# Forgetting attention with gate sums of keys only, fused maxima, late normalising and more units in flight

## The chip, the cores and the metric

The kernel runs on one core of one Trainium2 chip. The metric is the device time of one execution, in microseconds; three executions of the kernel before took 3905.02, 3905.59 and 3907.46 us. In the text PE is TensorE, DVE is VectorE, ACT is ScalarE, POOL is GpSimd, and SP is the queue that issues most DMAs.

## What is computed

The whole net is two blocks of two layers. Only one part is changed, the forgetting attention of the last layer: 512 tokens, 16 heads of width 64, causal, with a bias that is the difference of two running sums of a gate, F of the query's token and F of the key's.

```python
def forgetting_attention(h, w_q, w_o, k, v, F):
    q = (h @ w_q).reshape(b, s, B_HEADS, HEAD_DIM)
    def block(args):                      # 128 queries
        causal = q_pos[:, None] >= k_pos[None, :]
        decay = transpose(Fqb, (0, 2, 1))[..., None] - F_k[:, :, None, :]
        logits = einsum('bqhd,bkhd->bhqk', qb, k) * HEAD_DIM ** -0.5 + decay
        logits = where(causal, logits, -inf)
        p = softmax(logits, axis=-1)
        return einsum('bhqk,bkhd->bqhd', p, v)
    ...
    return o.reshape(b, s, B_WIDTH) @ w_o
```

Since the softmax runs over the keys, a term that depends on the query alone drops out of it.

## The kernel before

Activations lie with their channels on the partitions: a tile is 128 channels by 512 tokens. Large products take three matmuls for each 128 by 128 block of weights (`mm3`, lines 252 to 254): the weights are split into a rounded part `wh` (ACT, line 244) and the rest `wl` (DVE, line 245), the activations likewise. The split weights rotate through three buffers of four blocks each. `project` (line 361) is a generator: each step splits the weights of one output tile, 24 matmuls into one PSUM bank, and evacuates it.

The forgetting stage stands between two feed-forward parts. `norm2` makes its 8 input tiles (lines 323, 325 and 326). Then 8 pairs of heads follow. A pair has the query tile of its two heads, each on 64 partitions (`project`, evacuated on ACT at line 1415 as `q`), and four units, for the query blocks i = 3, 2, 1, 0, with 512, 384, 256 and 128 keys. At the first unit of a pair the gate sums of the keys are spread over all partitions, by four transposes (line 1470) and an ACT copy (line 1473, `fk`) per head.

A unit has `scores` and `values`. `scores` multiplies queries and keys (line 1427, the two heads in two banks), adds the gate sums (line 1432, DVE), adds the causal mask and takes the row maximum (line 1434, DVE), takes exponentials and their sums (line 1437, ACT), and normalises (lines 1438 and 1439, DVE). `values` transposes the weights on PE (`transposed`, lines 351 and 352, the copy on ACT), and multiplies them with the values (line 1454); the result of a pair gathers in one bank, `po`. `values` of a unit is written after `scores` of the next. After the 8 pairs, `out_project` multiplies the mixed tiles with the output weights.

The order on each engine is fixed when the program is built. A scheduler takes what it holds ready by its own costs, by the order of the code; `self.later()` gives the projections of the queries a lower priority than everything else. PSUM has eight banks: two with the tag `m` for projections, six with the tag `f` for all else. The three-matmul products here keep PE filled where heads leave gaps.

## Time and profile before

| | |
|---|---|
| median of three runs | 3905.59 us |
| span of the profiled execution, first to last instruction | 3901.2 us |
| PE busy, share of the span | 3663.6 us, 94% |
| DVE busy | 2172.9 us, 56% |
| ACT busy | 1445.6 us, 37% |
| POOL busy | 147.8 us, 4% |
| forgetting stage, first score matmul to end of the output projection | 3333.44 to 3514.33 us |
| in 3325 to 3515 us: DVE in line 1432, 1434, 1439 | 33.9, 30.2 and 24.5 us |
| in 3325 to 3515 us: ACT in line 1437, 352 | 35.5 and 26.1 us |

The page gives the span of the profiled execution and no time of its own beside it; the median lies 4.4 us above the span, which is what lies around the program. A granted clock of 1.00 is the full one of PE, 2.4 GHz, about half is its lower level of 1.2 GHz. A busy row of PE shows a matmul until its modelled end, while the next may start earlier, so the distance between two starts tells more than the length of a row.

### The profile page before, as it was taken

What the parts mean: (1) busy time and instruction counts of PE and PEld (TensorE: products, weight loads), DVE (VectorE), ACT (ScalarE), POOL (GpSimd) and SP (SyncE); (2) the same over time, 40 slices, a digit from 0 to 9 for tenths busy, and PEclk for the clock granted to TensorE, in tenths of its full rate; (3) what the DMA queues carried; (4) which work ended last, traced back from release to release, by engine and by line L of the source; (5) the groups of instructions that cost most, each with busy time, mean ns of one, the idle gap of its engine ahead of it and who ended that gap; (6) DMA issues with size and microseconds to landing.
All of it is one profiled execution on the core that took longest, in us unless ns stands there. A gap on an engine that the chain in (4) does not pass through costs nothing. (4 is left out here: it accounts for less than half of the span.)

```text
span 3901.2 us, 54964 instructions
## 1 busy us (share of the span) xinstructions
PE 3663.6 (94%) x21248; PEld 2659.1 (68%) x21248; DVE 2172.9 (56%) x5458; ACT 1445.6 (37%) x2827; POOL 147.8 (4%) x267
## 2 busy tenths in 40 slices
PE   7999998999899997988999998999989999999998
PEld 4777785333577775535888776788868888677887
DVE  5899874122688864215566665655643334764334
ACT  4566431111456631113233454323333233553222
POOL 0000000000000000000010000001100000000000
PEclk8999998999999997999999998999989999999999
DMA  5223254876433465995555321455522222012222
GB/s 203 70 80 101 77 196 167 327 275 259 156 111 109 135 215 199 356 356 179 194 194 189 113 76 54 142 193 205 191 80 97 96 94 95 33 52 79 97 102 81
DMA packets 154197, 588.04 MB, mean 151 GB/s; under 512 B 18048, under 2 KB 57256, under 8 KB 111952
## 3 DMA queue, kind: packets, MB, share of 16 engines
q1 hardware_dynamic: 113760, 442.43, 31.5%
q0 software_dynamic: 37872, 137.90, 10.5%
q10 hardware_dynamic: 2304, 4.20, 0.3%
q8 instruction: 167, 2.74, 0.3%
q14 instruction: 94, 0.77, 0.1%
HBM read 575.01 MB, written 9.46 MB: 150 GB/s over the span
## 5 line engine op out<-in xcount | busy, mean ns | idle before, releaser
L245 DVE TENSOR_TENSOR wl<-raw,wh 128x512 fp32r<-128x512 f32 (+1 forms) x826 | 558.3, 677 | 722.4 <-ACT wh L244 712.8
L244 ACT ACTIVATE wh<-raw 128x512 fp32r<-128x512 f32 (+1 forms) x826 | 512.1, 622 | 1203.2 <-PE m L253 835.1
L252 PE MATMUL m<-h,wh 128*128 128x512 f32 x1632 | 661.3, 406 | 30.6 <-DVE t L323 8.4
L253 PE MATMUL m<-h,wh 128*128 128x512 f32 x1632 | 658.3, 404 | 6.6 <-DVE h L326 5.2
L254 PE MATMUL m<-h,wl 128*128 128x512 f32 x1632 | 658.8, 404 | 1.1 <-DVE wl L245 1.1
L174 DVE SCALAR_TENSOR_TENSOR junk<-g,cb 128x512 bf16<-128x512 f32 (+1 forms) x440 | 374.1, 850 | 29.8 <-DMA g<-in_modT 17.5
L252 PEld LDWEIGHTS m<-h,wh 128*128 128x128 f32 x1632 | 315.4, 193 | 104.5 <-ACT h L325 19.1
L253 PEld LDWEIGHTS m<-h,wh 128*128 128x128 f32 x1632 | 313.8, 192 | 81.1 <-DVE h L326 16.3
L254 PEld LDWEIGHTS m<-h,wl 128*128 128x128 f32 x1632 | 313.9, 192 | 68.7 <-issue 6.9
L254 PE MATMUL m<-e,wl 128*128 128x512 f32 x832 | 325.7, 392 | 7.9 <-DVE wl L245 7.9
L252 PE MATMUL m<-e,wh 128*128 128x512 f32 x832 | 325.3, 391 | 0.5 <-ACT wh L244 0.5
L253 PE MATMUL m<-e,wh 128*128 128x512 f32 x832 | 324.9, 391 | 0.0
L252 PE MATMUL f<-h,wh 128*128 128x512 f32 x768 | 299.5, 390 | 0.0
L254 PE MATMUL f<-h,wl 128*128 128x512 f32 x768 | 299.1, 389 | 0.0
L253 PE MATMUL f<-h,wh 128*128 128x512 f32 x768 | 299.0, 389 | 0.0
L1106 PE MATMUL m<-raw,xg 128*64 128x512 f32 (+1 forms) x1264 | 258.5, 609 | 10.5 <-DMA raw<-in_exp_gu 10.5
L254 PEld LDWEIGHTS m<-e,wl 128*128 128x128 f32 x832 | 157.0, 189 | 40.9 <-DVE wl L245 8.3
L1106 PEld LDWEIGHTS m<-raw,xg 128*64 128x64 f32 (+1 forms) x1264 | 64.1, 126 | 175.0 <-issue 147.6
L252 PEld LDWEIGHTS m<-e,wh 128*128 128x128 f32 x832 | 157.2, 189 | 33.5 <-ACT wh L244 1.3
L253 PEld LDWEIGHTS m<-e,wh 128*128 128x128 f32 x832 | 157.0, 189 | 32.7
L252 PEld LDWEIGHTS f<-h,wh 128*128 128x128 f32 x768 | 144.5, 188 | 30.1 <-PE m L253 0.2
L254 PEld LDWEIGHTS f<-h,wl 128*128 128x128 f32 x768 | 144.3, 188 | 30.3 <-DVE wl L245 0.2
(455 smaller groups left out, 5170.0 us busy)
## 6 DMA issues: line engine op xcount, KB each, us to landing
raw<-in_exp_gu SPq DMA_DIRECT2D x98, 1024.0 KB, 6.6
raw<-in_ffn_in SPq DMA_DIRECT2D x88, 1024.0 KB, 4.8
g<-in_adaT POOLq DMA_DIRECT2D x144, 512.0 KB, 3.9
raw<-in_exp_dn SPq DMA_DIRECT2D x48, 1024.0 KB, 6.7
g<-in_modT POOLq DMA_DIRECT2D x80, 512.0 KB, 3.9
raw<-in_w_in SPq DMA_DIRECT2D x30, 1024.0 KB, 4.8
raw<-in_ffn_out SPq DMA_DIRECT2D x32, 896.0 KB, 4.6
raw<-in_ffn_out SPq DMA_DIRECT2D x16, 1024.0 KB, 4.7
```

The costliest lines, as they stand in the source:

```text
L174: self.paced(nc.vector.scalar_tensor_tensor(self.junk, before[0][:, js], 1.0, cb[:, js], op0=OP.mult, op1=OP.mult, accum_out=part[:, j:j + ...
L244: self.nc.scalar.activation(hi, src, AF.Copy)
L245: self.nc.vector.tensor_tensor(lo, src, hi.bitcast(F32), op=OP.subtract)
L252: nc.tensor.matmul(out, wh[k], hh[k], start=(first and k == ks[0]), stop=False)
L253: nc.tensor.matmul(out, wh[k], hl[k], start=False, stop=False)
L254: self.last = nc.tensor.matmul(out, wl[k], hh[k], start=False, stop=(last and k == ks[-1]))
L1106: self.nc.tensor.matmul(out[es, c:c + n], xg[:, es], t, start=start, stop=stop)
```

## The change

- The gate sum of the query's token is left out of the scores. What is added to a score is then minus the gate sum of the key, in a tile `bias` with two versions: plain, and with the causal triangle added to every block of 128 (the addition on GpSimd, line 1435). Each head has these in buffers that hold matrix-vector data in other stages (`g` and `cb`). `prepare` makes them, one pair ahead.
- One DVE instruction per part (line 1455) adds the bias to the scores out of PSUM and takes the maximum: one part without the triangle, one for the last 128 keys with it. A reduction (line 1457) joins the maxima of a unit's two heads, negated.
- The weights are not normalised. They are transposed as they are, and copied by ACT for one head (line 1477) and by DVE for the other (line 1475). The reciprocals of the sums of a whole pair are spread (line 1489, DVE), transposed by four matmuls (line 1493), copied (line 1496, ACT), and multiplied into the result of the pair (line 1498, DVE).
- PSUM: one bank `m`, four banks `s` for scores, two banks `f`, one bank `o` for the results.
- `values` stands two units behind `scores`; two projections are asked for before the loop, and one at the start of each pair.

```diff
-            with self.phase("forget", {"t": 3, "acc": 1, "q": 8, "fk": 3, "e": 4, "w": 3, "mix": 8}, {"m": 2, "f": 6}):
-                self.b2_consts()
+            with self.phase("forget", {"t": 4, "acc": 1, "q": 4, "fk": 2, "e": 6, "w": 4, "mix": 8},
+                            {"m": 1, "s": 4, "f": 2, "o": 1}):
...
+        def prepare(p):
+            for e in range(2):
+                b = self.bank()
+                for j in range(4):
+                    nc.tensor.transpose(b[:, j * 128:(j + 1) * 128],
+                                        self.Fq[:, j, 2 * p + e:2 * p + e + 1].to_broadcast([128, 128]), self.ident)
+                tag = ("g", "cb")[e]
+                t = bias[p, e] = self.gp.tile([128, 2, T], F32, tag=tag, name=tag)
+                nc.scalar.activation(t[:, 0], b, AF.Copy, scale=-1.0)
+                blocks = lambda u: u.rearrange("p (i m) -> p i m", m=128)
+                nc.gpsimd.tensor_tensor(blocks(t[:, 1]), blocks(t[:, 0]), tri.unsqueeze(1).to_broadcast([128, 4, 128]),
+                                        op=OP.add)
...
-                b = self.bank()
+                b = self.bank("s")
...
-                nc.vector.scalar_tensor_tensor(t[:, :n], fk[p, e][:, :n], self.Fq[:, i, hd:hd + 1], b[:, :n],
-                                               op0=OP.subtract, op1=OP.subtract, reverse1=True)
-                nc.vector.tensor_tensor_reduce(t[:, :n], t[:, :n], mask[:, 384 - 128 * i:512], 1.0, -3.0e38,
-                                               OP.add, OP.max, sm[:, 0:1])
-                nc.vector.tensor_scalar(sm[:, 1:2], sm[:, 0:1], -1.0, None, op0=OP.mult)
-                nc.scalar.activation(t[:, :n], t[:, :n], AF.Exp, bias=sm[:, 1:2], accum_out=sm[:, 2:3])
-                nc.vector.reciprocal(sm[:, 3:4], sm[:, 2:3])
-                nc.vector.tensor_scalar(t[:, :n], t[:, :n], sm[:, 3:4], None, op0=OP.mult)
-                P[p, i, e] = t
+                t = P[p, i, e] = self.tmp("e")
+                for part, cs in ((0, slice(0, n - 128)), (1, slice(n - 128, n))):
+                    if part or i:
+                        nc.vector.tensor_tensor_reduce(t[:, cs], b[:, cs], bias[p, e][:, part, cs], 1.0, -3.0e38, OP.add,
+                                                       OP.max, sm[:, 2 * e + part:2 * e + part + 1])
+            nc.vector.tensor_reduce(sm[:, 4:6], sm[:, 0:4].rearrange("p (e j) -> p e j", j=2), axis=AX.X, op=OP.max,
+                                    negate=True)
+            for e in range(2):
+                t = P[p, i, e]
+                nc.scalar.activation(t[:, :n], t[:, :n], AF.Exp, bias=sm[:, 4 + e:5 + e], accum_out=sums[p][:, i, e:e + 1])
...
+            if i == 1:
+                r = self.small(8).rearrange("p (i e) -> p i e", e=2)
+                nc.vector.reciprocal(r, sums[p])
+                sums[p] = self.tmp("t").rearrange("p (i e d) -> p i e d", e=2, d=64)
+                nc.vector.tensor_copy(sums[p], r.unsqueeze(3).to_broadcast([128, 4, 2, 64]))
             if i == 0:
+                b = self.bank()
+                for j in range(4):
+                    nc.tensor.transpose(b[:, j * 128:(j + 1) * 128], sums[p][:, j].rearrange("p e d -> p (e d)"),
+                                        self.ident)
+                rb = self.tmp("t")
+                nc.scalar.activation(rb, b, AF.Copy)
                 mix.append(self.tmp("mix"))
-                nc.scalar.activation(mix[p], po[p], AF.Copy)
+                nc.vector.tensor_mul(mix[p], po.pop(p), rb)
...
+        project_q(2)
+        prepare(0)
         units = [(p, i) for p in range(8) for i in (3, 2, 1, 0)]
+        ahead = 2
...
-        self.out_project(a["b_o"], mix, gate, st)
+        self.out_project(a["b_o"], mix, gate, st, "msfs")
```

What the change does to the order on the engines, at the places where a pair of heads begins. First PE in the kernel before, at the start of the pair of `q_28117`. In the names, `s` or `f` are score banks, `e` weights, `w` transposed weights, `m` projections, and a wait names the engine that ends it.

```order
L1470 MATMUL f_28126<-ident_75,Fq_24295 128x128
L1427 MATMUL f_28133<-k_24444,q_28117 128x512
L1427 MATMUL f_28135<-k_24444,q_28117 128x512 [waits PE_49]
L351 MATMUL f_28154<-ident_75,e_28054 128x128 [waits DVE_49,PE_49]
L351 MATMUL f_28158<-ident_75,e_28062 128x128 [waits DVE_49,Activation_49]
L1427 MATMUL f_28165<-k_24444,q_28117 128x384 [waits Activation_49]
L1454 MATMUL f_27989<-w_28153,vt_24722 64x128 [waits Activation_49]
L1454 MATMUL f_27989<-w_28157,vt_24722 64x128 [waits Activation_49]
L1427 MATMUL f_28167<-k_24444,q_28117 128x384 [waits DVE_49]
L252 MATMUL m_28290<-h_27448,wh_28282 128x512
```

The two 384-wide score matmuls are apart, and the next pair's projection follows them. The same place on PE now (`t_28180` are the spread reciprocals of the pair before):

```order
L253 MATMUL m_27750<-h_27491,wh_27746 128x512
L254 MATMUL m_27750<-h_27490,wl_27747 128x512
L1446 MATMUL s_28150<-k_24444,q_27775 128x512 [waits Activation_49]
L1446 MATMUL s_28152<-k_24444,q_27775 128x512
L1446 MATMUL s_28198<-k_24444,q_27775 128x384
L1446 MATMUL s_28200<-k_24444,q_27775 128x384
L1446 MATMUL s_28231<-k_24444,q_27775 128x256 [waits DVE_49,PE_49]
L1446 MATMUL s_28233<-k_24444,q_27775 128x256 [waits DVE_49,PE_49]
L1493 MATMUL f_28222<-ident_75,t_28180 128x128 [waits DVE_49]
L1493 MATMUL f_28222<-ident_75,t_28180 128x128 x3
L1472 MATMUL f_28247<-ident_75,e_28155 128x128 [waits Activation_49]
```

The projection into `m_27750`, which makes `q_27775`, ends right in front of the scores that read it; six score matmuls stand together, then the transposes of the reciprocals. ACT at that place, first before (around the copy that makes `q_28117`), then now:

```order
L1437 ACTIVATE e_28054,small_28055<-e_28054,small_28055 128x128 [waits DVE_49]
L352 ACTIVATE w_28070<-f_28071 128x256 [waits PE_49,Activation_49]
L1415 ACTIVATE q_28117<-m_28092 128x512
L1437 ACTIVATE e_28062,small_28063<-e_28062,small_28063 128x128 [waits DVE_49]
L352 ACTIVATE w_28075<-f_28076 128x256 [waits PE_49,Activation_49]
L1473 ACTIVATE fk_28124<-f_28119 128x512 [waits PE_49]
```

```order
L1477 ACTIVATE w_28212<-f_28213 128x128 [waits PE_49]
L244 ACTIVATE wh_27933<-raw_27927 128x512 [waits PE_49]
L244 ACTIVATE wh_28114<-raw_27927 128x512 [waits PE_49]
L1417 ACTIVATE q_27775<-m_27750 128x512 [waits PE_49]
L1461 ACTIVATE e_28155,small_28149<-e_28155,small_28154 128x512 [waits DVE_49]
L1461 ACTIVATE e_28158,small_28149<-e_28158,small_28154 128x512
```

The copy that makes the query tile moved from the middle of the pair before to its end, behind two splits of weights, of which `wh_28114` takes the buffer of `wh_27746`. DVE now, from the scores' arrival to the spread reciprocals:

```order
L245 TENSOR_TENSOR wl_28115<-raw_27927,wh_28114 128x512 [waits PE_49,Activation_49]
L1455 ISA e_28155,small_28154<-s_28150,g_28002 128x384 [waits PE_49]
L1455 ISA e_28155,small_28154<-s_28150,g_28002 128x128 [waits Pool_49]
L1455 ISA e_28158,small_28154<-s_28152,cb_28010 128x384 [waits PE_49]
L1455 ISA e_28158,small_28154<-s_28152,cb_28010 128x128 [waits Pool_49]
L1457 TENSOR_REDUCE small_28154<-small_28154 128x2 [waits DVE_49]
L1487 RECIPROCAL small_28178<-small_27964 128x8
L1455 ISA e_28203,small_28202<-s_28198,g_28002 128x256 [waits PE_49]
L1489 COPY t_28180<-small_28178 128x512 [waits DVE_49]
```

The copy that PE's line 1493 waits for stands behind five of the new pair's fused instructions; there is nothing like it before.

## Rows read from the trace of the kernel before

**Rows 1.** Table of stretches: start to end, length, busy of each engine, clock, DMA

```profile
3310.00:3320.00 10.00, 3.02 (x16) 2.54 (x16) 7.24 (x20) 3.54 (x6) 0.00 (x0) 0.60 0.00 0
...
3325.00:3515.00 190.00, 188.18 (x1055) 129.75 (x1055) 126.63 (x439) 107.91 (x271) 0.00 (x0) 0.99 0.13 45
```

**Rows 2.** Timeline of PE, stage's start: start, length, engine, line, operation, idle before

```profile
3323.85 1.09 PE L1470 MATMUL f<-ident,Fq 128*128 128x128 f32 x4 [8.00 <-DVE t L323]
3324.59 0.78 PE L252 MATMUL m<-h,wh 128*128 128x512 f32 x1
...
3333.44 1.77 PE L1427 MATMUL f<-k,q 64*128 64x512 f32 x8
3335.14 0.50 PE L254 MATMUL m<-h,wl 128*128 128x512 f32 x1
3335.48 0.40 PE L252 MATMUL m<-h,wh 128*128 128x512 f32 x1
3335.71 0.39 PE L253 MATMUL m<-h,wh 128*128 128x512 f32 x1
...
3340.15 1.22 PE L351 MATMUL f<-ident,e 128*128 128x128 f32 x8 [1.09 <-DVE small L1436]
```

**Rows 3.** Timeline of PE, second pair (a matmul of scores or values counts twice)

```profile
3351.15 1.13 PE L1427 MATMUL f<-k,q 64*128 64x512 f32 x4
3352.21 0.44 PE L351 MATMUL f<-ident,e 128*128 128x128 f32 x2
...
3353.79 0.91 PE L1427 MATMUL f<-k,q 64*128 64x384 f32 x2
3354.63 0.50 PE L253 MATMUL m<-h,wh 128*128 128x512 f32 x1
...
3359.65 0.43 PE L1454 MATMUL f<-w,vt 128*64 128x128 f32 x2
3360.01 0.70 PE L1427 MATMUL f<-k,q 64*128 64x256 f32 x4
3360.65 1.09 PE L1454 MATMUL f<-w,vt 128*64 128x128 f32 x14
3361.67 0.88 PE L351 MATMUL f<-ident,e 128*128 128x128 f32 x6
3362.47 0.48 PE L1427 MATMUL f<-k,q 64*128 64x128 f32 x2
```

**Rows 4.** Timeline of PE, the last pair's scores and the end of the stage

```profile
3462.44 1.13 PE L1427 MATMUL f<-k,q 64*128 64x512 f32 x4 [0.69 <-ACT q L1415]
...
3514.33 0.94 PE L289 MATMUL f<-ones,acc 128*128 128x1 f32 x8
```

**Rows 5.** Timeline of ACT ahead of the first scores

```profile
3332.23 0.63 ACT L244 ACTIVATE wh<-raw 128x512 fp32r<-128x512 f32 x1 [2.09 <-PE m L253]
3332.77 0.58 ACT L1415 ACTIVATE q<-m 128x512 f32<-128x512 f32 x1
```

**Rows 6.** Timeline of DVE, second and fourth pair

```profile
3352.38 0.75 DVE L1432 SCALAR_TENSOR_TENSOR e<-fk,Fq,f 128x512 f32<-128x512 f32 x1 [2.49 <-PE f L1427]
...
3389.25 0.69 DVE L1434 CUSTOM_DVE_ANT_0 e<-e,causal 128x512 f32<-128x512 f32 x1
...
3389.87 0.15 DVE L1436 TENSOR_SCALAR small<-small 128x1 f32<-128x1 f32 x1
```

**Rows 7.** Groups of DVE instructions by form: count, busy us, mean ns, idle before

```profile
L1317 DVE CUSTOM_DVE_ANT_0 e<-f,bias 128x384 f32<-128x384 f32 x16 | 8.8, 550 | 3.2 <-PE f L1313 3.2
L1317 DVE CUSTOM_DVE_ANT_0 e<-f,bias 128x256 f32<-128x256 f32 x16 | 6.3, 422 | 7.7 <-PE f L1313 7.7
L488 DVE COPY nt<-small 128x512 f32<-128x512 f32 x12 | 5.1, 421 | 0.0
L1317 DVE CUSTOM_DVE_ANT_0 e<-f,bias 128x128 f32<-128x128 f32 x16 | 4.4, 283 | 0.5 <-PE f L1313 0.5
```

**Rows 8.** Groups of POOL instructions by form: the longest kind

```profile
L992 POOL DMA_INDIRECT row<-scratch_h,idx x16 | 15.2, 947 | 401.1 <-PE f L1013 199.1 <-DVE ohf L973 90.9 <-PE m L862 55.2
```

More of the change, by code (lines that the diff above doesn't have):

```diff
@@ L1409, in forgetting @@
     def forgetting(self, h, k, v, gate, st):
-        nc, a, x = self.nc, self.a, self.x
+        nc, a = self.nc, self.a
         q = []
@@ L1448, in values @@
                 t = self.tmp("w").rearrange("p (j m) -> p j m", j=4)
-                self.transposed(t[:, :i + 1], P.pop((p, i, e)), i + 1)
+                b = self.bank()
+                for j in range(i + 1):
+                    nc.tensor.transpose(b[:, j * 128:(j + 1) * 128], P[p, i, e][:, j * 128:(j + 1) * 128], self.ident)
+                bv = b[:, :(i + 1) * 128].rearrange("p (j m) -> p j m", m=128)
+                if e:
+                    nc.vector.tensor_copy(t[:, :i + 1], bv)
+                else:
+                    nc.scalar.activation(t[:, :i + 1], bv, AF.Copy)
+                P.pop((p, i, e))
                 pt.append(t)
@@ L1455, in values, with project_q @@
                                      start=(i == 3 and j == 0), stop=(i == 0 and j == i), skip_group_check=True)
-            if i == 0:
-                mix.append(self.tmp("mix"))
-                nc.scalar.activation(mix[p], po[p], AF.Copy)
+            if i == 1:
[3 more added lines that the diff above has]
+                nc.vector.tensor_copy(sums[p], r.unsqueeze(3).to_broadcast([128, 4, 2, 64]))
+            if i == 0:
+                b = self.bank()
+                for j in range(4):
[3 more added lines that the diff above has]
+                nc.scalar.activation(rb, b, AF.Copy)
+                mix.append(self.tmp("mix"))
+                nc.vector.tensor_mul(mix[p], po.pop(p), rb)
+        def project_q(n=1):
+            with self.later():
+                for _ in range(n):
+                    next(cols, None)
+        project_q(2)
+        prepare(0)
         units = [(p, i) for p in range(8) for i in (3, 2, 1, 0)]
-        for n in range(len(units) + 1):
+        ahead = 2
+        for n in range(len(units) + ahead):
             if n < len(units):
@@ L1464, in forgetting @@
                 if i == 3:
-                    with self.later():
-                        next(cols)
-                    for e in range(2):
-                        b = self.bank()
-                        for j in range(4):
-                            nc.tensor.transpose(b[:, j * 128:(j + 1) * 128],
-                                                self.Fq[:, j, 2 * p + e:2 * p + e + 1].to_broadcast([128, 128]), self.ident)
-                        fk[p, e] = self.tmp("fk")
-                        nc.scalar.activation(fk[p, e], b, AF.Copy)
+                    project_q()
+                if i == 2 and p < 7:
+                    prepare(p + 1)
                 scores(p, i)
-            if n:
-                values(*units[n - 1])
-        self.out_project(a["b_o"], mix, gate, st)
+            if n >= ahead:
+                values(*units[n - ahead])
+        self.out_project(a["b_o"], mix, gate, st, "msfs")
     def norm1(self, l, n, x, r):
```

18 lines of the change are left out of this document (11 added, 7 removed).

## Prediction

> **What bounds the kernel now.** I read the table of stretches first. In the forgetting stage TensorE (PE) is busy for 188.18 of 190 us at a granted clock of 0.99, VectorE (DVE) for 126.63 and ScalarE (ACT) for 107.91 [rows 1]. So PE bounds the stage, and idle time of the others costs nothing. Then the timeline of PE. A busy row does not tell what a matmul costs there, since each is shown until its modelled end and the next starts earlier; I price by the distance from one start to the next. The first score matmul starts at 3333.44, the output projection ends at 3514.33 [rows 2, 4]: 180.9 us. In these PE waits visibly twice, 1.09 for the first weights to transpose [rows 2] and 0.69 for a query tile [rows 4]. The remaining 179.1 us I call PE's own work. The edits that relieve DVE and ACT can therefore give back at most 1.8 us; all else must come from PE's own work, or be lost in new waits.
>
> **DVE and ACT edits (gate sums dropped, fused add and max, no normalising).** For each pair of heads DVE loses eight additions of 0.75 us (512 columns) and less, and eight scalings. All of that lies beside a full PE: 0 us. Without that cover the additions alone would be worth up to 8 x 0.75 = 6 us a pair [rows 6]. The fused instruction is already in this kernel at L1317, reading PSUM: 0.55, 0.42 and 0.28 us for 384, 256 and 128 columns [rows 7]. The two extra units in flight remove the one wait of 1.1 us.
>
> **PE's own work.** From the order of instructions I count matmuls and stretches of one kind.
> 1. Scores. The two heads of a unit use different halves of the rows. Side by side, both 512s take 1.06 us, but a lone 384 takes 0.84 [rows 3], and in the first pair, where both 512s and both 384s follow each other, all four take 1.70 [rows 2], so that the joined 384s cost 0.64, and joined 256s would cost 0.43. The old order tears the 384s apart in seven pairs (1.06 + 0.84 + 0.84 + 0.64 for the 256s [rows 3] = 3.38). The new one has 512, 512, 384, 384, 256, 256 in a row: 1.70 + 0.43 = 2.13. That is 1.25 x 7 = 8.7 us less; the first pair and two others, which also tore the 256s, give some 2 more: -10.7.
> 2. Transposes of the row sums: 4 a pair, 32 in all. Six transposes take 0.80 [rows 3], some 0.11 each without the restart: +3.5.
> 3. Value matmuls: 53 stretches become 63, mostly one more lone matmul a pair at 0.36 [rows 3]: +3.6.
> 4. Projection matmuls (384 as before) fall into 51 stretches instead of 36. The first of a stretch takes 0.34 where the next takes 0.23 [rows 2], and the step out of it may cost as much again: 15 x 0.11 to 15 x 0.28; I take 4.0, since the stretches are mostly of one to three.
> Sum: +0.4 us, with -4 and +4 as bounds.
>
> What the rows show of changes between kinds of matmul is a restart: 0.84 for a lone 384 against 0.64 for joined ones, 0.34 against 0.23 for a projection's first matmul [rows 2, 3]. The Trainium skill (TensorEngine Tiling (Array Packing), Key Properties) says that a change of tiling mode drains TensorE. By that alone the 12 more stretches (209 for 197) would cost 12 x 0.2 = 2.4 us where my items give 0.4; the whole would come out 2 us later.
>
> **The start.** Before, two groups of gate transposes stand ahead of the projection; the second waits until 3323.85 for the bank that the norm still reads, the projection starts at 3324.59, and the first score matmul at 3333.44 [rows 2]. After, four groups stand there on two banks. The third needs ACT's copy of the first, which stands on ACT behind all eight norm tiles, the fourth the second's copy: about 3325.0 and 3325.7. The projection starts at 3326.5, its first 8 matmuls at the lower clock, at 0.43 each, then 16 at 0.23, and scores begin at about 3334.7: +1.2 (0 to 2).
>
> **A new wait ahead of each pair: the query tile.** "Projections ahead" does not come out of the order: the projections yield to everything, have one bank for two, and each ends right in front of the score matmuls that need it. On ACT a weight split (L244) stands before the copy that makes the query tile, and waits for the last but one projection matmul. The start of the stage has this sequence: the split at 3332.23, the copy 0.54 later, the first score matmul 0.67 after that [rows 2, 5]. The last but one matmul ends some 0.2 after the last has started (0.39 long, begun 0.23 earlier [rows 2]), so scores start 0.2 + 0.54 + 0.67 = 1.41 after it, where an unbroken stream would take 0.33: 1.1 a pair. Without the split it is the 0.69 of [rows 4]; with a late ACT 1.4. Seven pairs (the first is in the start): 7.7 us (4.9 to 9.8). Queued behind are all of the pair's scores, and DVE, which waits for them.
>
> **A second new wait: the row sums.** Behind the six joined score matmuls PE's order has four transposes of the spread reciprocals of the pair before (L1493). They wait for a DVE copy (L1489) which on DVE stands behind the new scores' own maxima. Counted from the first score matmul: DVE gets them 1.23 later (3352.38 after 3351.15 [rows 3, 6]). Two heads of 384 and 128 columns, each row less the 0.07 by which DVE's instructions overlap (0.69 long, next after 0.62 [rows 6]): 2 x (0.48 + 0.21) to 2.61; a small reduction and a reciprocal (0.15 each [rows 6], with a wait between) to 2.85; 256 columns 0.35 to 3.20; the copy, priced by L488 at 0.42 [rows 7], to 3.62. PE is there at 2.13, waits until 3.67: 1.5 us. With whole durations it is 1.9; with scores coming 0.3 earlier 1.2. Seven pairs: 10.5 us (8.4 to 13.3). In the first pair there is no such transpose, but the 256s and the 128s wait for their four banks: 0.9 (0 to 2). I followed the rest of a pair the same way: first values at 6.4 against weights at 5.8, second half at 7.9 against 6.8; nothing else is late. If the heads did not run side by side, the six would take longer and this wait be shorter by as much.
>
> **Nothing:** GpSimd's (POOL) two additions of 512 columns a pair have no row. They start about 13.5 us into a pair and are needed at 22, so each may take 4 us; DVE's like-sized rows are under 0.8, POOL's longest kind 0.95 [rows 8]. The Trainium skill (GPSIMD Engine Reference, Elementwise) has 4497 ns for four times the columns, as an estimate 1.1 us each; the sum would not move. The last pair's output projection has 13 matmuls, 3.0 us, ahead of the one that needs the last mixed tile, about as long as copy, product and split take: 0.
>
> **Sum.** +0.4 - 1.8 + 1.2 + 7.7 + 0.9 + 10.5 = +18.9 us. The profiled span is 3901.2; the median of the runs, 3905.59, lies 4.4 above it, for what lies around the program, and that stays. So 3905.6 + 18.9, about 3924. With all low ends 3913 (-4 - 1.8 + 4.9 + 8.4), with all high ones 3935.
>
> **Rivals.**
> - No measurable difference: the waits come, but are half as long, because score results reach DVE before the whole group has ended and ACT passes the query copy ahead. At 0.6 for each of 14 waits: +0.4 - 1.8 + 8.4, with the start 3912 to 3914 at most, and nearer 3908 with own work at its low side. For it: the old order shows such waits only twice. Against: the queues' order is fixed and the DVE chain is a sum of rows.
> - Faster: PE's waits stay as rare as before and splitting costs nothing: -10.7 + 3.5 - 1.8 = -9, 3897. It decides on the two chains: both must end before PE arrives, so each pair needs some 2.6 us of cover that no row shows.
> - The clock falls: at 3310 to 3320, where PE was busy for 3 of 10 us, the granted clock was 0.60 [rows 1], and matmuls took 0.43 for 0.23. Two gaps within 5 us of each pair could do that for as long: 5 x (1 - 0.23/0.43) = 2.3, x 7 = 16 more, 3940. Against: the stage with its two waits kept 0.99 [rows 1].
>
> **How the numbers follow.** The forecast 0.62 (3913 to 3935), no difference 0.17, faster 0.11, clock 0.10. A measurement tells about 0.2%, 7.8 us, from no change. Slower: 0.62 + 0.10 = 0.72. The range, 3904 to 3938, takes in the forecast's bounds, most of the no-difference case and the edge of the clock's.
>
> **What would show it.** Right: PE idle for about 1 us before the first score matmul of each pair, released by ACT's query copy, and about 1.5 us before L1493, released by DVE; pairs of some 20.5 us instead of 18.5 (3351.15 to 3462.44 holds six [rows 3, 4]); joined score matmuls; clock 1.00. Wrong: a stage as long as before with neither gap, or gaps in front of the value matmuls or at POOL.

## The result, and the profile after

The changed kernel takes 3929.76 us (median of 4 runs, 3923.38 to 3935.90) against 3906.53 for the kernel before: a ratio of 1.0054, with an interval of 1.0041 to 1.0067. Forecast were 3924, slower, in a range of 3904 to 3938. The profiled execution has a span of 3926.3 us, 25.1 more than the 3901.2 before.

To place the 25.1 I cut both traces at the same instructions: the row-spread transposes L303 of the norm ahead of the stage and those of the norm behind it. Between them lies what I call the stage.

| | before | after | difference |
|---|---|---|---|
| start of the program to L303 | 3313.88 | 3318.64 | +4.8 |
| L303 to the first score matmul | 19.55 | 21.37 | +1.8 |
| first score to the end of the out-projection | 180.89 | 199.56 | +18.7 |
| out-projection to the next L303 | 5.17 | 4.95 | -0.2 |
| behind the stage | 381.67 | 381.76 | +0.1 |

The stage itself is 225.88 us for 205.61: +20.3. The 4.8 ahead of it are not the change's: TensorE's order there is the same, and in the 13 traces of this study L303 came at anything between 3313.9 and 3326.3.

The waits of TensorE (PE) from the first score to the end of the stage: who waited, for what, us in total, times, longest.

```profile
PE s L1446 <- ACT q L1417: 7.9, 8, 1.0
PE s L1446 <- DVE small L1455: 2.5, 8, 0.3
PE f L1493 <- DVE t L1489: 1.3, 7, 0.2
```

The table of stretches, which answers to [rows 1]:

```profile
3325.00:3340.00 15.00, 9.22 (x32) 7.39 (x32) 6.64 (x11) 6.36 (x12) 5.48 (x4) 0.66 0.09 27
3340.00:3540.00 200.00, 189.15 (x1053) 127.18 (x1053) 93.25 (x372) 91.91 (x233) 15.05 (x12) 1.00 0.12 41
```

VectorE (DVE) went from 126.63 of 190 us [rows 1] to 93.25 of 200, and it brought nothing. The clock stayed at 1.00. The timeline of PE at the stage's start, where [rows 2] have the kernel before:

```profile
3318.64 1.12 PE L303 MATMUL f<-ident,small 128*128 128x128 f32 x4 [2.23 <-DVE small L280]
3319.55 1.91 PE L1429 MATMUL f<-ident,Fq 128*128 128x128 f32 x8
3329.76 1.97 PE L1429 MATMUL f<-ident,Fq 128*128 128x128 f32 x8 [8.29 <-ACT g L1433]
3331.37 0.78 PE L252 MATMUL m<-h,wh 128*128 128x512 f32 x1
...
3340.01 1.77 PE L1446 MATMUL s<-k,q 64*128 64x512 f32 x8 [1.03 <-ACT q L1417]
3342.09 1.89 PE L1446 MATMUL s<-k,q 64*128 64x256 f32 x6 [0.31 <-DVE small L1455]
```

And a pair in the middle, where [rows 3] have one of before. Scores count twice. Five pairs running start 20.67 apart, where those of before lie 16.7 to 18.9 apart (the last 21.7).

```profile
3378.94 0.39 PE L254 MATMUL m<-h,wl 128*128 128x512 f32 x1
3380.30 1.77 PE L1446 MATMUL s<-k,q 64*128 64x512 f32 x8 [0.98 <-ACT q L1417]
3382.39 1.36 PE L1446 MATMUL s<-k,q 64*128 64x256 f32 x4 [0.31 <-DVE small L1455]
3383.92 0.66 PE L1493 MATMUL f<-ident,t 128*128 128x128 f32 x4 [0.18 <-DVE t L1489]
3384.41 0.60 PE L1472 MATMUL f<-ident,e 128*128 128x128 f32 x4
```

From the start of the last projection matmul to the first score it is 1.36; in an unbroken stream the next starts 0.33 later. So the query tile costs 1.03 a pair. ScalarE (ACT) does the split, then the copy, as [rows 5] had it:

```profile
3379.14 0.63 ACT L244 ACTIVATE wh<-raw 128x512 fp32r<-128x512 f32 x1 [2.68 <-PE m L253]
3379.67 0.58 ACT L1417 ACTIVATE q<-m 128x512 f32<-128x512 f32 x1
```

From the first score to L1493 it is 3.62, where the forecast had 3.67. The six joined scores alone would take 2.13, so 1.49 is lost by that count, although only 0.31 + 0.18 is shown as idle. The rest hides in the row of 1.36 us: its two 256-column scores stand apart. The same timeline, opened at the second one, and beside it DVE's (the read-outs of 0.08 us, L1455's second instructions, end a part):

```profile
3383.08 0.67 PE L1446 MATMUL s<-k,q 64*128 64x256 f32 x2
```

```profile
3381.47 0.56 DVE L1455 CUSTOM_DVE_ANT_0 e<-s,g 128x384 f32<-128x384 f32 x1 [0.97 <-PE s L1446]
3381.95 0.08 DVE L1455 DVE_READ_ACCUMULATOR2_ANT small<- 128x1 f32 x1
3381.95 0.28 DVE L1455 CUSTOM_DVE_ANT_0 e<-s,g 128x128 f32<-128x128 f32 x1
3382.16 0.08 DVE L1455 DVE_READ_ACCUMULATOR2_ANT small<- 128x1 f32 x1
3382.16 0.55 DVE L1455 CUSTOM_DVE_ANT_0 e<-s,cb 128x384 f32<-128x384 f32 x1
...
3382.85 0.08 DVE L1455 DVE_READ_ACCUMULATOR2_ANT small<- 128x1 f32 x1
...
3383.45 0.42 DVE L1489 COPY t<-small 128x512 f32<-128x512 f32 x1
```

DVE's last read-out of the first head's 512 columns is at 3382.16 and of the second's at 3382.85, 0.69 later. The 256s start 0.23 after each, at 3382.39 and 3383.08. There are four score banks: the 512s and 384s fill them, and each 256 waits until DVE has emptied one. L1493 comes last and adds 0.18.

So two theories stand for what the change costs. **Two chains**: the query tile (ACT) and DVE behind the score banks, with PE's own work about as before. **Own work**: of the 11.7 us that the three waits show 10.7 lie behind the first score, the old waits gone give back 1.8, and most of the 9.8 that are then missing from the 18.7 is PE's own work in 240 stretches of one kind for 200 (weights, row sums and gates counted as three kinds of transpose, and each width of scores as a kind; the prediction, with one kind of each, had 209 for 197). Inside the first theory it is open whether the row sums hold PE, as the prediction had it, or the banks.

### The profile page after: what moved, and what is told of

It is laid out like the page before. It is cut to its first block, busy times and chain, and to the rows that moved or that the text cites. A ratio compares the mean times of both kernels' runs of the same rounds, so it can differ in the third digit from the quotient of the medians.

```text
span 3926.3 us, 54985 instructions
## 1 busy us (share of the span) xinstructions
PE 3677.7 (94%) x21280; PEld 2666.9 (68%) x21280; DVE 2142.5 (55%) x5394; ACT 1432.8 (36%) x2795; POOL 168.4 (4%) x283
## 4 chain that ended last, share of the span: by engine, by line
PE 71%; DVE 10%; issue 8%; DMA 7%; ACT 3%; SPq 1%; POOL 0%; POOLq 0%; ACTq 0%; DVEq 0%
PE m L252 12%; PE m L253 12%; PE m L254 12%; PE m L1106 9%; PE f L252 4%; PE f L253 4%; PE f L254 4%; DMA c<-in_exp_gu 1%; PE f L1054 1%; DMA g<-in_modT 1%; PE s L760 1%; DVE t L323 1%; DMA raw<-in_exp_dn 1%; DMA g<-in_adaT 1%; PE f L351 1%
## 5 line engine op out<-in xcount | busy, mean ns | idle before, releaser
L252 PE MATMUL m<-h,wh 128*128 128x512 f32 x1616 | 655.9, 406 | 30.9 <-DVE t L323 8.4
L252 PE MATMUL f<-h,wh 128*128 128x512 f32 x752 | 293.3, 390 | 0.0
L253 PE MATMUL f<-h,wh 128*128 128x512 f32 x752 | 292.8, 389 | 0.0
L252 PEld LDWEIGHTS m<-e,wh 128*128 128x128 f32 x832 | 156.9, 189 | 33.6 <-ACT wh L244 1.3
L1106 PE MATMUL m<-raw,eh 128*64 128x512 f32 (+1 forms) x640 | 156.4, 617 | 7.8 <-DMA raw<-in_exp_dn 7.8
```

Of the source, the lines that this page charges most:

```text
L252: nc.tensor.matmul(out, wh[k], hh[k], start=(first and k == ks[0]), stop=False)
L253: nc.tensor.matmul(out, wh[k], hl[k], start=False, stop=False)
L1106: self.nc.tensor.matmul(out[es, c:c + n], xg[:, es], t, start=start, stop=stop)
```

## The experiments

Stage is L303 to L303; main is the part from the first score to the end of the out-projection; ahead is how many projection matmuls of the queries stand before the first score. Own is worked out: main less the idle time of PE shown in it, plus 0.227 us (one start to the next) for each projection matmul done ahead (in r_early, q_on_dve and before_ahead it holds some microseconds at the lower clock). The ratio is to the kernel before, run beside it.

| run | time | ratio (interval) | stage | main | ahead | own |
|---|---|---|---|---|---|---|
| before, its profile | 3906.53 | | 205.61 | 180.89 | 29 | 185.6 |
| after | 3929.76 | 1.0054 (1.0041 to 1.0067) | 225.88 | 199.56 | 24 | 194.2 |
| after_again | 3931.55 | 1.0053 (1.0036 to 1.0070) | 224.81 | 199.51 | 24 | 194.1 |
| r_early | 3929.85 | 1.0056 (1.0038 to 1.0074) | 226.75 | 201.37 | 24 | 194.4 |
| q_on_dve | 3929.85 | 1.0051 (1.0031 to 1.0070) | 225.12 | 199.96 | 24 | 195.8 |
| f_shared | 3914.79 | 1.0013 (1.0004 to 1.0023) | 208.92 | 190.29 | 24 | 187.6 |
| banks_shared | 3915.87 | 1.0017 (1.0006 to 1.0028) | 210.35 | 185.60 | 29 | 186.3 |
| no_yield | 3906.98 | 0.9996 (0.9986 to 1.0006) | 204.92 | 180.61 | 48 | 190.7 |
| shared_no_yield | 3906.36 | 0.9992 (0.9983 to 1.0002) | 203.68 | 174.36 | 72 | 186.7 |
| own_order | 3902.03 | 0.9983 (0.9973 to 0.9992) | 196.63 | 167.18 | 72 | 179.8 |
| own_order_m1 | 3905.57 | 0.9988 (0.9979 to 0.9997) | 200.13 | 175.83 | 48 | 185.5 |
| before_ahead | 3909.57 | 1.0000 (0.9989 to 1.0010) | 205.40 | 175.86 | 72 | 188.3 |
| fused_only | 3909.25 | 0.9996 (0.9987 to 1.0005) | 205.92 | 181.02 | 29 | 184.9 |

Single times of one kernel lie up to 17 us apart; the stage of the changed kernel repeats within 1.1. I judge by the stage, and by main only between runs with like projections ahead.

A second table splits main by what PE worked on: the time from a matmul's start to the next one's, without idle time, added up by kind. For projections it is what they took above 0.227 us each, and in brackets the number of stretches into which they fall. The last column counts changes of shape, places where the next matmul uses the array of PE in another shape: scores use half of the rows (64\*128 in the views), values half of the columns (128\*64), projections and transposes all of it (128\*128).

| run | idle | projections above 0.227 | scores of 512 and 384 | of 256 | of 128 | transposes, weights and gates | transposes, row sums | values | changes of shape |
|---|---|---|---|---|---|---|---|---|---|
| before | 1.8 | 5.9 (35) | 20.9 | 6.9 | 5.8 | 28.3 | | 30.7 | 151 |
| after | 10.8 | 10.2 (50) | 14.2 | 10.7 | 6.6 | 28.0 | 4.0 | 33.4 | 171 |
| f_shared | 8.2 | 4.0 (17) | 16.0 | 9.5 | 3.4 | 31.1 | 4.4 | 32.0 | 163 |
| banks_shared | 5.9 | 5.7 (25) | 17.0 | 9.3 | 3.4 | 29.3 | 4.4 | 30.0 | 151 |
| no_yield | 0.8 | 6.2 (31) | 20.8 | 7.7 | 3.6 | 30.0 | 4.9 | 30.5 | 176 |
| shared_no_yield | 4.0 | 4.8 (24) | 18.1 | 9.3 | 3.4 | 29.2 | 4.4 | 30.3 | 153 |
| own_order | 3.7 | 5.1 (25) | 18.1 | 5.0 | 3.4 | 27.6 | 5.2 | 28.4 | 135 |
| own_order_m1 | 1.2 | 2.9 (15) | 18.1 | 7.9 | 3.5 | 30.9 | 5.1 | 30.0 | 154 |
| before_ahead | 3.9 | 7.3 (43) | 20.9 | 6.1 | 6.8 | 28.6 | | 31.5 | 154 |
| fused_only | 2.7 | 12.1 (77) | 17.1 | 5.1 | 3.4 | 26.7 | | 33.3 | 162 |

**The changed kernel again.**

> The changed kernel once more, unedited, to see how far its stage repeats: its four first times lay 12.5 us apart (3923.4 to 3935.9). If the spread comes from outside the stage: 225.9 us again, within 1, with the stage's beginning elsewhere than at 3318.6. If the granted clock falls inside the stage in some executions, as it did twice in the run with the early row sums (3 us longer pairs at a granted 0.5): up to 229, with pairs of 23 us among those of 20.67.

The stage is 224.81, with pairs of 20.67 as before and the three waits to the tenth; the 1.1 is in the start, where the granted clock rose at another time. The stage began at 3324.2. The spread comes from outside.

**Row sums early (r_early).**

```diff
-            if i == 1:
+            if i == 2:
                 r = self.small(8).rearrange("p (i e) -> p i e", e=2)
                 nc.vector.reciprocal(r, sums[p])
```

> The changed kernel with one edit: the reciprocals of the row sums and their spread copy are written one unit earlier, so that VectorE has them done ahead of the next pair's maxima; TensorE's order has their transposes at the end of the pair, no longer behind the six new scores. The stage (from the row-spread transposes L303 of the norm ahead to those of the norm behind) is 225.9 us in the changed kernel and 205.6 in the kernel before. Theory as predicted (the row sums hold TensorE for 1.5 us a pair): the stage loses 7 x 1.5 = 10.5, to about 215.5; transposes then start 2.1 us after the first score matmul. Rival, banks (the new trace shows the two 256-column scores 0.69 apart, VectorE's pace for one head, each waiting for one of the four score banks; the row sums add only the last 0.2 to 0.3): the stage loses 2 to 3.5, to 222.4 to 224; the 256s are still 0.69 apart and the next transposes start 3.3 to 3.4 after the first score. Rival, own work (what is not shown as idle is the price of 240 stretches for 200): 23 stretches fewer at 0.2, 5 us less, about 221, with the 256s joined.

The same pair in its timeline of PE, and then two stretches of it (the ninth value is the granted clock):

```profile
3380.80 1.77 PE L1446 MATMUL s<-k,q 64*128 64x512 f32 x8 [0.98 <-ACT q L1417]
3382.88 1.36 PE L1446 MATMUL s<-k,q 64*128 64x256 f32 x4 [0.31 <-DVE small L1455]
3384.52 0.66 PE L1472 MATMUL f<-ident,e 128*128 128x128 f32 x4 [0.28 <-ACT e L1461]
```

```profile
3345.00:3405.00 60.00, 55.06 (x336) 36.06 (x335) 26.38 (x121) 27.42 (x75) 8.65 (x6) 0.98 0.05 19
3405.00:3412.00 7.00, 7.00 (x33) 5.05 (x34) 2.19 (x13) 4.13 (x14) 0.00 (x0) 0.54 0.00 0
```

With no row sums behind the scores the 256s stand as far apart as before, and the next transposes start at 3.72 instead of 3.62, now held by exponentials. So the row sums did not hold PE for 1.5 us: the banks did. An undisturbed pair takes 19.79, 0.88 less: 0.39 because the weights' transposes now come at 3.72 where they came at 4.11, and 0.49 in the rest of the pair, which has fewer stretches now. Seven times 0.88 is 6.2, more than the 3.5 expected for banks and near the 5 for own work, but the stage did not get it. At 3405 to 3412 the granted clock was 0.54 with PE busy throughout, and the pair around it took 22.85; it fell so at 3344 and at 3487 too. The 10.5 that I expected with the prediction is excluded; own work is not yet.

**Query copy on VectorE (q_on_dve).**

```diff
-            nc.scalar.activation(q[f], b, AF.Copy, scale=0.125)
+            nc.vector.tensor_scalar(q[f], b, 0.125, None, op0=OP.mult)
```

> The changed kernel with the query tile copied out of its bank by VectorE instead of ScalarE; TensorE's order is the same word for word. Theory as predicted (ScalarE does a weight split of 0.54 us between the last but one projection matmul and the copy): without it the wait ahead of a pair falls from 1.0 to 0.69, the size of the same wait in the kernel before: -0.3 x 8 = -2.4, the stage at 223.5 us. Rival (the split is done in time and the 1.0 is the copy and the semaphores alone): 1.0 again, the stage at 226. If VectorE has its own half of the split ahead of the copy: 1.0 or more as well, then with that row ahead of it.

```profile
PE s L1446 <- DVE q L1417: 6.4, 8, 0.9
PE s L1446 <- DVE small L1455: 2.5, 8, 0.3
PE f L1493 <- DVE t L1489: 1.3, 7, 0.2
```

The wait is 0.8 for 1.0, where 0.69 was expected; pairs are 0.18 shorter, and the rest is as it was. The split ahead of the copy cost 0.2 of the 1.0; the copy and what lies between it and its neighbours are the rest. Taking ACT out was worth some 0.2 us a pair; what takes the wait away is distance from the projection, as no_yield and own_order show.

**Banks and order.** Four runs undo the banks or the yielding of the projections. In f_shared scores and transposes share six banks; in banks_shared there are two for projections and value sums share the six too ("m": 2, "f": 6, as before):

```diff
-                            {"m": 1, "s": 4, "f": 2, "o": 1}):
+                            {"m": 1, "f": 6, "o": 1}):
...
-                b = self.bank("s")
+                b = self.bank()
```

> The changed kernel with scores and transposes sharing six banks (in place of four and two); one bank for projections and one for value sums stay. In TensorE's order each pair still has its last projection matmul right ahead of its first score, but other work stands between the 512-, 384- and 256-column scores. It takes away the wait behind the score banks alone. Theory (two chains): the query waits stay, eight of 1.0 us shown idle, 1.04 over an unbroken stream; the stage comes out 6 us above the 210.4 of the run that shares banks and has two for projections: 215 to 218, that is 8 to 11 below the changed kernel's 225.9. Rival (the score banks were not the cost; the second projection bank made all of the gain of that run): 223 to 227. Rival (the query wait costs nothing in itself): 209 to 212.

> The changed kernel with the banks of before: two for projections and six that scores, transposes and value sums share, in place of one, four, two and one. TensorE's order then has six matmuls between the last projection matmul and the first score matmul of a pair in five pairs of eight (one in the changed kernel), and other work between 512-, 384- and 256-column scores. Theory (two chains, query tile and VectorE behind the score banks, make the loss): query waits of 1.0 us in three pairs instead of eight, -5; the wait for banks and row sums of 1.5 a pair gone in seven pairs, -10; torn scores +4 to +8.7: the stage at 213 to 219 us, device time about 3917 to 3923. Rival, own work (row-sum transposes and stretches cost the rest): 188 stretches for 240 at 0.2 each less 10 on top of the visible waits of 11.7: the stage at about 204, device time about 3908. If neither wait matters: 226.

f_shared, waits of PE from the first score on, and PE at the stage's start:

```profile
PE f L1446 <- ACT q L1417: 7.9, 8, 1.0
PE f L1472 <- ACT e L1461: 0.5, 1, 0.5
PE o L1483 <- ACT w L1477: 0.4, 1, 0.4
```

```profile
3320.50 1.92 PE L1429 MATMUL f<-ident,Fq 128*128 128x128 f32 x8
3322.30 0.79 PE L252 MATMUL m<-h,wh 128*128 128x512 f32 x1
```

All eight query waits stay and the waits behind DVE are gone. The stage lost 17.0, more than the 8 to 11 expected, and 7.7 of it lie in the start, which I had not counted: only two groups of gate transposes stand ahead of the projection, none waits 8.3 us for a bank that ACT empties behind the norm, and the projection starts at 3322.30, 2.7 after L303 instead of 12.7.

Main is 9.3 shorter, which looks like the expected price of the banks, but the second table puts it elsewhere: 2.7 less idle, 6.2 less for projections that fall into 17 stretches and not 50, 3.2 less for 128s that now stand side by side, against some 3 more for transposes. The 256s gained 1.1 alone, since other work stands between their two heads now, and a lone one takes 0.62, as the distance of these two starts shows, where both side by side take 0.63 (5.0 for eight pairs in own_order):

```profile
3393.60 0.70 PE L1446 MATMUL f<-k,q 64*128 64x256 f32 x2
3394.22 0.43 PE L1483 MATMUL o<-w,vt 128*64 128x128 f32 x2
```

banks_shared has the start wait again (8.0 us), two query waits for eight, and a main another 4.7 lower: 2.3 less idle, 1.1 for five projection matmuls done ahead, 2.0 less for values. With both, the stage loses 15.5 of its 20.3. Own work had 204 here, the chains 213 to 219; 210.4 lies between. Neither run gives the price of the banks by itself, since PE's order changed with them.

no_yield keeps the changed kernel's banks and drops the yielding:

```diff
-            with self.later():
-                for _ in range(n):
-                    next(cols, None)
+            for _ in range(n):
+                next(cols, None)
```

> The changed kernel with the query projections at their place in the code, not giving way to all else: TensorE's order then has 27 to 147 matmuls between the last projection matmul of a pair's queries and its first score. Theory: no query wait, -7.9 us of shown idle; other work stands between the score matmuls, so the wait behind the banks shrinks too, by up to 10; scores torn, +5 to +9; projections are no longer filler in every pair's end and new waits for exponentials may show, 0 to +8: the stage at 212 to 226 us, most likely 218. Rival (the query wait is cover for something else that then ends late, DVE or ACT): the stage stays at 224 to 228 although no matmul waits for a query tile any more.

```profile
PE o L1483 <- ACT w L1477: 0.5, 1, 0.5
```

That is the only wait left in main. The stage is 204.92, below the expected 212 and where it was before the change. PE's own work is 190.7 in this order, 5.1 above before, and 4.9 of it are the row sums' transposes; its 384s and 256s are torn apart as those of before are (all scores 32.0 us for 33.6). What it won over the changed kernel is 10.0 of idle, 8 us of idle at the start that its 48 projection matmuls fill, and some 7 us in projections and values.

**A version faster than both (own_order).** Three edits: banks_shared, no_yield, and the row sums' reciprocals and transposes two units earlier.

```diff
-            if i == 1:
+            if i == 2:
                 r = self.small(8).rearrange("p (i e) -> p i e", e=2)
...
-            if i == 0:
+            if i == 1:
                 b = self.bank()
                 for j in range(4):
                     nc.tensor.transpose(b[:, j * 128:(j + 1) * 128], sums[p][:, j].rearrange("p e d -> p (e d)"),
                                         self.ident)
-                rb = self.tmp("t")
+                rb = sums[p] = self.tmp("t")
                 nc.scalar.activation(rb, b, AF.Copy)
+            if i == 0:
                 mix.append(self.tmp("mix"))
-                nc.vector.tensor_mul(mix[p], po.pop(p), rb)
+                nc.vector.tensor_mul(mix[p], po.pop(p), sums[p])
```

> The changed kernel with three edits: the banks of before (two for projections, six shared), query projections that give way to nothing, and the row sums' reciprocals, their transposes and the copy two units earlier, so that only the product is left at a pair's end. In TensorE's order no score follows its projection closely (52 or more matmuls between), 172 stretches against 240 in the changed kernel and 200 before, the 256-column scores side by side. Theory (the changed kernel's units cost TensorE no more than those of before, and only the two chains made it slower): the stage at 197 to 204 us against 205.6 before, device time 3898 to 3906. Rival (whatever leaves one chain enters another: exponentials or maxima late for the transposes): the stage at 205 to 212, device time 3906 to 3914, with idle time ahead of weight transposes.

Its waits, and PE around a pair's first score:

```profile
PE f L1446 <- DVE small L1455: 2.2, 6, 0.4
PE f L1472 <- ACT e L1461: 0.7, 1, 0.7
```

```profile
3393.53 0.39 PE L254 MATMUL m<-h,wl 128*128 128x512 f32 x1
3393.85 1.13 PE L1446 MATMUL f<-k,q 64*128 64x512 f32 x4
3394.91 0.66 PE L1472 MATMUL f<-ident,e 128*128 128x128 f32 x4
```

The scores start 0.32 after the projection matmul ahead of them, which belongs to a later pair. The stage is 196.63, 9.0 less than before, and the time 0.17% lower (interval 0.08 to 0.27). Two runs take it apart. shared_no_yield leaves the row sums where the change put them:

> The changed kernel with two of the three edits: the banks of before and query projections that give way to nothing; the row sums stay where the changed kernel has them, behind the 384-column scores of the next pair. TensorE's order: 189 stretches, 256-column scores apart. It undoes the early row sums of the run at 196.6 us. Theory (row sums in the middle of the next pair's scores tear the 256s apart and make TensorE wait for VectorE's copy): a pair some 0.7 to 1.0 us longer than there (17.27), the stage at 201 to 204 us. Rival (row sums are free once banks are shared): 196 to 198.

203.68, with pairs of 18.49 for 17.27: the row sums in the middle of the next pair's scores cost 1.2 a pair, 7.1 in all. They do it by order, not by a wait (idle is 4.0 for 3.7): the torn 256s take 4.3 more, the values 2.0 more. own_order_m1 has own_order's edits with f_shared's banks:

> As the run with three edits, but with one bank for projections, one for value sums and six shared by scores and transposes. 176 stretches. Theory: with no query close to its scores the single projection bank costs only within a projection's own start, 0 to 3 us: the stage at 198 to 206, device time 3899 to 3908. Rival (one projection bank holds up the out-projection or the next pair's queries): the stage at 206 to 214.

200.13, as expected: one bank for projections and one for value sums cost 3.5 here, with no query wait at all. By the second table the 256s take 2.9 more, the transposes 3.3 and the values 1.6, with 2.5 less idle and 2.2 less for projections.

before_ahead asks whether the projections alone do it. It is the kernel before, with two of them ahead of the first pair and none yielding:

```diff
+        next(cols), next(cols)
         for n in range(len(units) + 1):
...
-                    with self.later():
-                        next(cols)
+                    next(cols, None)
```

> The kernel before with one edit: two query projections ahead of the first pair, and none of them gives way to other work (as in the run with its three edits on the changed kernel). Scores, weights, sums, banks and units as before. It tells what of that run's 9 us is due to the projections alone. Theory (the gain was the idle 8.0 us of the norm's bank at the start, now filled by projections, and the one query wait of 0.7; the rest came from the changed kernel's scores side by side): the stage at 198 to 203 us against 205.6, device time lower than before by 3 to 8. Rival (the gain belongs to the changed kernel's order alone): 205 to 208. Rival (the projections alone make all of it): 195 to 198.

205.40: nothing, against my 198 to 203. It has the start of own_order (24.34 and 24.41) and the same projections done by then, but main is 175.86 for 167.18, both with 72 projection matmuls ahead. So most of own_order's 8.7 comes from the changed kernel's units in another order, not from the projections: scores take 7.4 less and values 3.1 less, row sums' transposes 5.2 more. As an estimate 1.7 of the 8.7 are not the order's: in before_ahead the granted clock fell to half for 3.4 us, at 3475.

**The VectorE edits alone (fused_only).** Query gate sums dropped, add and max fused, GpSimd's bias and projections ahead stay; weights are normalised as before, with the banks of before and one unit ahead.

```diff
-        ahead = 2
+        ahead = 1
...
+                nc.vector.reciprocal(rc := self.small(1), sums[p][:, i, e:e + 1])
+                nc.vector.tensor_scalar(t[:, :n], t[:, :n], rc, None, op0=OP.mult)
```

> Of the change only the edits for VectorE and GpSimd: query gate sums dropped, add and max fused, the bias with its triangle made by GpSimd, and projections begun ahead; weights normalised by VectorE as before, banks as before, one unit ahead as before, no transposes of row sums. TensorE's order has 253 stretches against 200 before; scores of one length stand side by side. Theory (these edits lie beside a full TensorE and are worth nothing; what moves the time is TensorE's order): scores joined -8, stretches of projections and values +4 to +8, one query wait of 1.0 us in the two pairs with one matmul in between: the stage at 202 to 208 us, device time 3902 to 3911. Rival (VectorE's relief itself shortens the stage): below 200. Rival (each change between kinds of matmul costs 0.2 us): 53 more stretches, +10, less the joined scores: 208 to 214.

205.92 and a ratio of 0.9996: no difference, as expected. It is a sum of gains and losses in PE's order, not of edits without any effect: joined scores took 8.0 us less than before, projections in 77 stretches for 35 took 6.2 more, values 2.6 more. The relief of VectorE brought PE no time: it sat idle 2.7 us for 1.8.

The run also speaks on own work. At 0.2 us for each change between kinds the stage would have been 208 to 214. But of the changes that it adds only 11 are changes of shape (162 for 151); most are between projections and transposes. A few of its rows show what a step costs, from one start to the next:

```profile
3388.43 0.50 PE L253 MATMUL m<-h,wh 128*128 128x512 f32 x1
3388.77 0.39 PE L254 MATMUL m<-h,wl 128*128 128x512 f32 x1
3389.00 0.49 PE L1474 MATMUL f<-ident,e 128*128 128x128 f32 x3
3389.25 0.47 PE L252 MATMUL m<-h,wh 128*128 128x512 f32 x1
3389.56 0.39 PE L253 MATMUL m<-h,wh 128*128 128x512 f32 x1
3389.79 0.49 PE L1474 MATMUL f<-ident,e 128*128 128x128 f32 x3
3390.21 0.43 PE L1485 MATMUL f<-w,vt 128*64 128x128 f32 x2
```

Three transposes take 0.25 to a projection, whose first matmul then takes 0.31; together that is what three transposes at 0.11 and one projection matmul at 0.23 take in an unbroken stream. So this change of kind costs nothing. Three transposes take 0.42 to a value, which uses the array in another shape, and the first projection behind values takes 0.34 (3388.43 to 3388.77). In the traces of before, after and five other runs each step to another shape cost about 0.1 us on leaving, and the first projection matmul behind it another 0.11. What has a price in these rows is the change of shape, not that of kind.

That leaves the 8.6 us by which own stands higher in the changed kernel (194.2 for 185.6). By the second table 6.2 of them are the banks' doing: the 256s take 10.7 where they take 5.0 side by side (own_order; 5.1 here), and the 512s and 384s in front of them 1.77 a pair for the 1.70 of [rows 2]. PE is busy for most of this time, not waiting: a bank that comes 0.69 after the other tears the two heads apart, and each then takes 0.62 alone. The other 2.4 is PE's own work: 4.0 more for row sums' transposes, 4.3 for projections and 2.7 for values, 8.3 less for the scores and 0.3 less for the other transposes. Both theories hold a part of the 18.7: the chains cost 16.9 (10.7 idle and 6.2 torn scores), own work 2.4, five projection matmuls fewer ahead 1.1, and the old waits that are gone give back 1.8.

## Why the prediction came out

**What bounds the stage.** Right. DVE lost a quarter of its work and the stage grew; in fused_only the relief brought PE no time.

**PE's own work, +0.4.** Measured +2.4, within the bounds of 4, with items that missed both ways: row sums' transposes 4.0 for 3.5, projections 4.3 for 4.0, values 2.7 for 3.6. The joined scores did come, but gave back 8.3 for 10.7 even without what the banks took. The 256s were priced at 0.43, without the step to the next kind (0.63 with it), and the 128s, which are torn apart in all pairs now, were not in the sum (+0.8).

The Trainium skill (TensorEngine Tiling (Array Packing), Key Properties) says that a change of tiling mode drains TensorE. The traces agree: each change of shape has a price in them, and a change between projections and transposes, of one shape, has none. The prediction's 2.4 by that rule was the nearer sum, but by luck: it counted 12 more stretches at 0.2, where there are 20 more changes of shape (171 for 151).

**The start, +1.2.** +1.8, and +0.8 in after_again. The mechanism was right (L1429 waits for ACT's copy behind the norm). What I took for given is the larger thing: 8 us of idle stand there before and after, each time for a bank, and f_shared has none of them.

**The query tile, 1.1 a pair, 7.7.** Right in place, releaser and size: 1.03, 7.2 in seven pairs. The split had less part in it than I said: 0.2.

**The row sums, 1.5 a pair, 10.5.** Near in size, wrong in cause. The time from first score to L1493 was 3.62 for my 3.67, since both are the same chain of DVE's rows: 1.17, two heads of 0.69, reduction, copy. But I had the six scores run through to 2.13 and then 1.5 of idle for the copy L1489, and that sign did not show: the idle there is 0.18. The scores are held before that, for banks that the same DVE instructions free. The step that failed is that I followed the banks in the first pair alone ("for their four banks", 0.9) and not in the others. r_early shows the difference: moving the row sums away leaves the 256s where they were and does not win the 10.5.

The size is a little smaller too. Of the 1.49 a pair, 0.49 is idle and 0.77 goes to torn scores; the rest is the step from joined scores to the next kind, which 2.13 left out. Seven pairs of 1.26 and 1.1 in the first make 9.9, where 10.5 + 0.9 were forecast. The Trainium skill has a general form: TensorEngine Tiling (Array Packing), PSUM Bottleneck, says that packing the array speeds up TensorE but not the emptying of its banks. The trace agrees: two heads side by side give 0.53 us a head of 512 columns, DVE takes 0.69.

**Nothing at GpSimd (POOL).** Right. Its additions took 1.27 us each, the first 1.78, and nobody waited for them. The estimate from the Trainium skill (GPSIMD Engine Reference, Elementwise) was 1.1; the trace is a little above it.

```profile
L1435 POOL TENSOR_TENSOR g<-g,tri 128x512 f32<-128x512 f32 x8 | 10.7, 1339 | 599.0 <-DVE h L326 490.8 <-ACT g L1433 108.2
L1435 POOL TENSOR_TENSOR cb<-cb,tri 128x512 f32<-128x512 f32 x8 | 10.1, 1267 | 0.0
```

**The sum.** 18.9 forecast, 20.3 in the stage: own work 2.4 for 0.4, banks and row sums 9.9 for 11.4, the query tile 7.2 for 7.7, the start 1.8 for 1.2, the old waits as forecast, and 1.1 for the five projection matmuls, which had no term. So part of the closeness is luck: misses of up to 2 us cancel. The medians differ by 23.2 in the first runs and by 22.0 in after_again's; what lies above 20.3 is less than the spread of the work ahead of the stage.

**The rivals.** No difference: the waits are of full size. Faster: not this kernel, and the condition named, both chains gone, is not enough: no_yield has 0.8 us of idle in main and ends 0.7 below before. own_order, 9.0 below, has its scores side by side as well. The clock: not in the changed kernel, where it held 1.00 with three gaps of 1 us or less in each pair; r_early shows that it can fall with gaps like these, twice for 7 us, and one pair came out 3 us longer by it.

## What to carry to other kernels

Follow each bank, not only each result: when scores are packed side by side, the time in which the reader empties one bank sets the pace as soon as the banks are full, and a loss of 1.3 us a pair may show as 0.5 of idle, because two matmuls that come apart keep PE busy for longer than side by side. Work that yields to everything ends right in front of whoever needs it, however early it is written, so count in the order how many instructions lie between a result and its first use. A run that changes banks changes the order too, so split its gain by kind of work before putting it down to the banks. And relief of an engine that is not the bound is worth only what the better order that it allows is worth: the change gave +20.3 us as it stands, -0.7 without yielding (no_yield) and -9.0 in own_order.

## What had not been expected of the hardware

- A step between matmuls of different shapes costs PE time, one between kinds of the same shape none: three transposes took 0.42 us to a value and 0.25 to a projection (fused_only, 3389).
- Two 256-column scores of different row halves took 0.63 us side by side and 0.62 each when apart (own_order, f_shared).
- A granted clock of 0.54 for 7 us in the middle of a stretch in which PE was busy throughout (r_early, 3405 to 3412). The gaps ahead of it, 0.98, 0.31 and 0.28 us, stand in every pair of that run, and it fell in three of them; in q_on_dve and before_ahead it fell once each, for 3.4 us. What sets it off stays open.
- Work with the same instructions in the same order ahead of the stage took 3313.9 to 3326.3 us in 13 profiled executions, more than four times the 2.7 us by which the first four times of the kernel before differ. For a change of 0.2% the stage's own time decides.
